# A hybrid decoder layer on one core: the opening's spread of c by transposes, and the recurrence gates as products over 64 rows, two halves of the channels at a time

## The chip, the core and the metric

The kernel runs on one core of a Trainium2 chip. Its time is the device time of one execution in microseconds. The engines are named as in the profile: PE (TensorE, matrix products; PEld are its weight loads), DVE (VectorE), ACT (ScalarE), POOL (GpSimd) and SP, which issues the DMA transfers. Times inside a profile are microseconds from the first instruction of the profiled execution.

## The reference, cut to what matters

One layer over x of 512 positions by 1024 channels, with a condition vector c of 1024. All data are float32.

```python
c_act = silu(c)
shift, scale, gate = split(c_act @ w_mod + b_mod, 3)
h = rmsnorm(x, norm_gain) * (1 + scale) + shift
q, k, v, z_attn, x_lru, z_lru = split(h @ w_in, 6)            # each 512 wide
attn = block_attention(rope(q), rope(k), v)                   # 8 heads of 64, causal
y_attn = rmsnorm(attn, attn_out_gain) * silu(z_attn)
xc = causal_depthwise_conv(x_lru, conv_w, conv_b)             # width 4
r = sigmoid(xc @ blockdiag(w_r) + b_r)                        # 8 blocks of 64 x 64
i = sigmoid(xc @ blockdiag(w_i) + b_i)
a = exp(-8 * r * softplus(-lam))
rec = scan(a, sqrt(1 - a * a) * i * xc)                       # h[t] = a[t] h[t-1] + u[t]
y_lru = rmsnorm(rec, lru_out_gain) * silu(z_lru)
out = rmsnorm(x + gate * (concat(y_attn, y_lru) @ w_out), final_gain)
```

## The kernel before

**Order.** Nothing is emitted where it is written. The function `op` records an operation with its engine, a cost, the buffers it reads and writes and a due time; `Plan.emit` (L97) then lays all operations out in one order per engine, with the costs as durations, taking at each engine the ready operation that is due first, and hands buffers out as they come free. The order on each engine is thus fixed when the program is built, and each engine's queue runs in that order. An operation with `alt` may go to either of two engines (PSUM copies to ACT or DVE). Constants such as `NWARM`, `SPACE`, `GATE0`, `DECAY0` shift due times. PSUM has 8 banks of 128 x 512; buffers marked "side" (scores, transposes, attention outputs, gate products) may hold at most 6 of them.

**Precision.** A product of two float32 matrices is done as three products of a high and a low part (`mm3`, L242 to L245): each operand is split by an ACT (or DVE) copy into the high part and a DVE subtraction into the low part (`split`, L247).

**Opening.** Eleven rows of 128 numbers (c and three columns of vectors) are loaded as `first`. ACT takes silu of the eight rows of c into `crow` (L320). PE turns `first` into columns (L325). For the modulation, silu(c) must stand in a row on all 128 partitions (`cb`): eight products of 8 contraction rows (L336), each with a column of the identity repeated 128 times, write it into two PSUM banks, which are copied out. `NWARM` products (L312) of a constant tile, whose result nobody reads, fill PE's queue until the first real work. Around them the queue holds four transposes (L416) of the first 128 channels of normalised x, one per 128 positions.

**First stage (L407 to L432).** For each of the 8 slices d of the channels: DVE multiplies the modulation weights by `cb` and sums along the row, which gives the two columns `g` (scale and shift; L384 for d = 0, L396 after); PE transposes x into a bank `xp` (L412); ACT makes `h = xp * scale + shift`, once as the high part (`h0h`, `h1h`, ...) and once whole, DVE the low part (`h0l`, ...); and PE does 21 products of 128 x 128 by 128 x 512 (L431) into seven banks `acc`. The weights `w0...` are split as above. Then 17 units follow (`UNITS`), each of 24 products for 128 further columns of the input projection (L693), `v` in one block of 96.

**Beside the units.** Attention runs in six blocks: scores (L570) as products over 32 rows, four of them on the four row strips of the array at a time, into four banks; softmax on DVE (L583) and ACT (L586, L597); transposes (L633) copied to `pt`; and the products with v (L616). The recurrence takes 4 chunks of 128 channels (two blocks of 64 each): `conv` (L487), then the two gates. Their weights `wg` are eight 128 x 128 matrices, one for each chunk and gate, each with two 64 x 64 blocks on its diagonal and zeros elsewhere. The gates are 3 products each (L500), so 24 in all, into a bank `gr` and a bank `gi` per chunk. ACT takes tanh of `gi` (L503); `gr` stays in its bank until `decay` (L509), which takes sigmoid of all four straight out of PSUM (L512) after one table load, and then the exponentials. `recur` does the scan.

**End.** The output projection (`po`), 16 groups of 12 products, is multiplied, added and normalised, and goes out.

Of the kernel before, what the change touches and what calls it, by code (L numbers as in the profile page):

```python
# [7 lines left out]
F32 = mybir.dt.float32  # L8
# [3 lines left out]
OP = mybir.AluOpType  # L12
# [9 lines left out]
NFIRST = 7  # L22
NWARM = 31
CUTS = (((0, 768), (768, 1024)), ((0, 512), (512, 1024)))
# [4 lines left out]
V_C = 72  # L29
NV = 80  # L30
UNITS = ["x3", "v0", "v1", "v2", "v3", "k2", "k3", "q2", "q3", "a0", "a1", "l0", "l1", "l2", "l3", "a2", "a3"]
SPACE = 14.0
BY_TANH = ("a0", "a1", "a2", "a3", "l0", "l1", "l2", "l3")
GATE0, GATE_STEP, DECAY0, REC0 = 32.0, 3.0, 44.0, 84.0

# [142 lines left out]
def tile_hymba_block(ctx: ExitStack, tc: tile.TileContext, x, ws0, wss, wgt, win0, wv, winr,  # L178
# [132 lines left out]
    for n in range(NWARM):  # L311
# [3 lines left out]

    epsc, ones, junk, crow = fix("epsc", [128, 1]), fix("ones", [128, 1]), fix("junk", [128, 1]), fix("crow", [ND, 128])
    op("V", 0.1, lambda: V.memset(epsc[:], EPS), [], [epsc], -20)
    op("V", 0.1, lambda: V.memset(ones[:], 1.0), [], [ones], 0)
    op("A", 0.1, lambda: A.activation(junk[:], epsc[:], AF.Silu), [epsc], [junk], -6, "silu")
    op("A", 0.1, lambda: A.activation(crow[:], first[0:ND, :], AF.Silu), [first, junk], [crow], -5, "silu")  # L320
    op("A", 0.1, lambda: A.activation(junk[:], epsc[:], AF.Sqrt), [epsc, crow], [junk], -4, "sqrt")


    ps, v0 = bank("v0"), fix("v0", [128, 3])
    op("PE", 0.2, lambda ps=ps: PE.transpose(ps[:, 0:11], first[:], ident[0:11, 0:11]), [first, ident], [ps], 1)  # L325
    op("V", 0.2, lambda ps=ps: (V.tensor_copy(v0[:, 0:2], ps[:, ND:ND + 2]), V.tensor_scalar(
        v0[:, 2:3], ps[:, ND + 2:ND + 3], 1.0, None, op0=OP.add)), [ps], [v0], 2)
    cb = t4("cb")
    for half in range(2):
        ps = bank("cp")  # L330
        s = slice(half * 512, (half + 1) * 512)

        def spread(ps=ps, half=half):
            for j in range(4):
                k = half * 4 + j
                PE.matmul(ps[:, j * 128:(j + 1) * 128], ident[0:ND, k:k + 1].to_broadcast([ND, 128]), crow[:], start=True, stop=True)  # L336
        op("PE", 0.8, spread, [crow, ident], [ps], 2)
        copy(512, lambda s=s: cb[:, s], lambda ps=ps: ps[:], [ps], [cb], 4.5 + 0.5 * half, True)
# [37 lines left out]
    def gain(d):  # L376

        sc, g = col("sc"), col("g")
        half = (sc, sch)
        for j in (1, 0):  # L380
            if d == 0:
                for n in range(2):
                    lo, up = CUTS[j][n]
                    op("V", dv(up - lo), lambda j=j, n=n, lo=lo, up=up: V.scalar_tensor_tensor(  # L384
                        ws[0][j][n][:], ws[0][j][n][:], 1.0, cb[:, lo:up], op0=OP.mult, op1=OP.mult,
                        accum_out=half[n][:, j:j + 1]), [ws[0][j][n], cb], [ws[0][j][n], half[n]], 8 - 2 * j + 0.7 * n)
                    if j and not n:
                        op("V", 0.1, lambda: V.tensor_add(sc[:, 1:2], sc[:, 1:2], v0[:, 2:3]), [sc, v0], [sc], 9.2)
                if j:
                    op("V", 0.2, lambda: V.tensor_scalar(g[:, 1:2], sch[:, 1:2], sc[:, 1:2], v0[:, 0:1],  # L390
                                                         op0=OP.add, op1=OP.mult), [sc, sch, v0], [g], 9.4)
                else:
                    op("V", 0.15, lambda: V.scalar_tensor_tensor(g[:, 0:1], sc[:, 0:1], v0[:, 1:2], sch[:, 0:1],
                                                                    op0=OP.add, op1=OP.add), [sc, sch, v0], [g], 9.5)
                continue
            op("V", dv(1024), lambda j=j: V.scalar_tensor_tensor(  # L396
                part(d, j), part(d, j), 1.0, cb[:], op0=OP.mult, op1=OP.mult, accum_out=sc[:, j:j + 1]),
               [ws[d][j], cb], [ws[d][j], sc])
        if d == 0:
            return g  # L400
        op("V", 0.2, lambda: V.tensor_scalar(
            g[:, 1:2], sc[:, 1:2], vec[:, V_SCALE + d:V_SCALE + d + 1], vec[:, V_GAIN + d:V_GAIN + d + 1],
            op0=OP.add, op1=OP.mult), [sc, vec], [g])
        op("V", 0.1, lambda: V.tensor_add(g[:, 0:1], sc[:, 0:1], vec[:, V_SHIFT + d:V_SHIFT + d + 1]), [sc, vec], [g])
        return g
# [81 lines left out]
    def conv(ps, ch, due, gate_due):  # L487
        xl, xc = t2("xl"), t2("xc")
        copy(512, lambda: xl[:], lambda: ps[:], [ps], [xl], due, True)
        w = lambda k: vec[:, V_CW + 4 * ch + k:V_CW + 4 * ch + k + 1]  # L490
        op("A", ac(512, 2), lambda: A.activation(xc[:], xl[:], AF.Identity, bias=vec[:, V_CB + ch:V_CB + ch + 1],
                                                 scale=w(3)), [xl, vec], [xc])
        for k in (2, 1, 0):
            s = 3 - k
            op("V", dv(512, 1), lambda k=k, s=s: V.scalar_tensor_tensor(  # L495
                xc[:, s:], xl[:, :S - s], w(k), xc[:, s:], op0=OP.mult, op1=OP.add), [xl, xc, vec], [xc])
        hi, lo = split(xc, t2, f"xc{ch}", 512)
        pr, pi, i = bank("gr", "side"), bank("gi", "side"), t2("gi")
        for ps2, n in ((pi, 2 * ch + 1), (pr, 2 * ch)):
            op("PE", 3 * pe(512), lambda n=n, ps2=ps2: mm3(  # L500
                ps2[:], wgs["h"][:, n], wgs["l"][:, n], hi[:], lo[:], True, True),
               [wgs["h"], wgs["l"], hi, lo], [ps2], gate_due + (0 if n % 2 else 2))
        op("A", acp(512, 1), lambda: A.activation(i[:], pi[:], AF.Tanh, bias=halves[:, ch:ch + 1], scale=0.5), [pi, halves], [i],  # L503
           gate_due + 2, "exp")
        op("V", dv(512), lambda: V.scalar_tensor_tensor(i[:], i[:], 1.0, xc[:], op0=OP.add, op1=OP.mult), [i, xc], [i],
           gate_due + 8)
        REC[ch] = (pr, i)

    def decay(chs, due):  # L509

        rs, prs = [t2("gr") for _ in chs], [REC[ch][0] for ch in chs]
        op("A", len(chs) * acp(512, 1), lambda: [A.activation(  # L512
            r[:], ps[:], AF.Sigmoid, bias=vec[:, V_BR + ch:V_BR + ch + 1]) for r, ps, ch in zip(rs, prs, chs)],
           [vec, *prs], rs, due, "sigmoid")
        for n, (r, ch) in enumerate(zip(rs, chs)):
# [180 lines left out]

    wgr = t4("wg", F32, (128, 8, 128))
    load(wgr, wg, T_REST + 2)
    wgs["h"], wgs["l"] = split(wgr, like(wgr), "wg", 1024)

# [22 lines left out]
    for u, name in enumerate(UNITS):  # L723
# [7 lines left out]
        elif kind == "x":  # L731
            conv(ps, idx, t1 + 1, T_REST + GATE0 + GATE_STEP * idx)
            decay(range(4), T_REST + DECAY0)
            for n in range(4):
# [180 lines left out]
```

## Time and profile before

| | |
|---|---|
| median of 3 runs | 238.06 us (237.94 to 239.41) |
| the profiled execution | 238.57 us, span 236.5 us |
| PE | 229.0 us busy (97%), 1236 products |
| DVE | 203.8 us busy (86%) |
| ACT | 139.3 us busy (59%) |
| POOL | 9.5 us busy (4%) |
| DMA | 38.54 MB, 163 GB/s over the span |

The span runs from the first to the last instruction; the device time is 2.07 us longer. A line of the timeline gives the start, the time that its instructions take together, the engine, the line of the kernel, the operation, and what it writes and reads; "x8" means eight instructions of that kind in a row. In the chain of waits each piece of time is given once, to the instruction that the end of the program waited for, so that its durations add up.

### The profile page before, as it was taken

To read this page: it belongs to the slowest core of one execution; us is meant where nothing else is said; L and a number is where in the kernel's file an instruction comes from. 1 tells how busy PE (TensorE), PEld (TensorE's weight loads), DVE (VectorE), ACT (ScalarE), POOL (GpSimd) and SP (SyncE) were. 2 spreads that over 40 slices of the span, in tenths; PEclk is the share of its full clock that TensorE was granted. 3 is DMA by queue.
4 is the path that set the end of the run, shared out by engine and by line. 5 is a ranking of instruction groups with operands and counts; after the bars stand their busy time and mean duration, and the time that the engine had idled before them with its cause. 6 is when DMAs were issued, how large, how long until landed. Compare 5 with 4: busy or idle time off the path is not lost.

```text
span 236.5 us, 3435 instructions
## 1 busy us (share of the span) xinstructions
PE 229.0 (97%) x1236; PEld 181.2 (77%) x1236; DVE 203.8 (86%) x396; ACT 139.3 (59%) x263; POOL 9.5 (4%) x32
## 2 busy tenths in 40 slices
PE   7999999999999999999999999999999999999990
PEld 5457888888888788786788887878887788888890
DVE  1679998895999899899999999989998999956583
ACT  7859464652659587799992347766374711303363
POOL 1010000057000000000000000000000000000000
PEclk9999999999999999999999999999999999999997
DMA  6999999822045223755122354474521000000044
GB/s 232 378 418 417 416 418 423 327 91 89 11 169 177 89 89 103 256 191 167 61 118 89 92 190 180 166 256 190 177 89 65 26 0 3 0 0 0 0 180 177
DMA packets 11782, 38.54 MB, mean 163 GB/s; under 512 B 1515, under 2 KB 1782, under 8 KB 11638
## 3 DMA queue, kind: packets, MB, share of 16 engines
q1 hardware_dynamic: 11600, 38.06, 43.5%
q10 hardware_dynamic: 166, 0.27, 0.3%
q8 instruction: 10, 0.16, 0.3%
q14 instruction: 6, 0.05, 0.1%
HBM read 36.22 MB, written 2.10 MB: 162 GB/s over the span
## 4 chain that ended last, share of the span: by engine, by line
PE 96%; ACT 1%; DVE 1%; issue 0%
PE acc L431 17%; PE pj L243 14%; PE pj L245 13%; PE pj L244 13%; PE po L243 6%; PE po L245 6%; PE po L244 6%; PE spare L312 4%; PE av L616 4%; PE sc L570 4%; PE tp L633 4%; PE cp L336 2%; PE xp L412 1%; PE ss L758 1%; PE gi L243 0%; PE gi L245 0%
## 5 line engine op out<-in xcount | busy, mean ns | idle before, releaser
L586 ACT ACTIVATE z<-z,mn 128x128 f32<-128x128 f32 (+3 forms) x32 | 17.7, 554 | 7.9 <-DVE mn L583 7.2
L396 DVE SCALAR_TENSOR_TENSOR ws<-ws,cb 128x1024 f32<-128x1024 f32 x14 | 16.9, 1219 | 0.4 <-DMA ws<-in_wss_dram 0.4
L583 DVE CUSTOM_DVE_ANT_0 z<-sc,cst 128x128 f32<-128x128 f32 (+3 forms) x32 | 14.2, 487 | 1.6 <-PE sc L570 1.6
L233 ACT COPY pt<-tp 128x128 f32<-128x128 f32 (+3 forms) x26 | 8.5, 391 | 6.2 <-PE tp L633 6.2
L312 PE MATMUL spare<-warm 128*128 128x512 bf16 x31 | 10.2, 486 | 1.5 <-DVE warm L310 1.5
L796 DVE SCALAR_TENSOR_TENSOR xr<-po,rba,xr 128x512 f32<-128x512 f32 (+2 forms) x9 | 6.2, 692 | 6.2 <-PE po L245 6.0
L807 ACT ACTIVATE o<-xr 128x512 f32<-128x512 f32 x7 | 4.4, 635 | 12.0 <-DVE xr L796 12.0
L633 PE MATMUL tp<-ident,z 128*128 128x128 f32 x80 | 10.5, 272 | 0.0
L633 PEld LDWEIGHTS tp<-ident,z 128*128 128x128 f32 x80 | 9.4, 140 | 1.4
L778 DVE TENSOR_TENSOR wo<-wo,grow 128x1024 f32<-128x1024 f32 x8 | 9.8, 1219 | 0.0
L541 DVE SCALAR_TENSOR_TENSOR wgt<-wgt,cb 128x1024 f32<-128x1024 f32 x8 | 9.7, 1218 | 0.0
L495 DVE SCALAR_TENSOR_TENSOR xc<-xl,vec,xc 128x511 f32<-128x511 f32 (+2 forms) x12 | 9.0, 747 | 0.2
L616 PE MATMUL av<-pt,v 128*64 128x512 f32 (+3 forms) x64 | 9.1, 436 | 0.0
L312 PEld LDWEIGHTS <-warm 128*128 128x128 bf16 x31 | 3.5, 118 | 6.1 <-issue 2.9
L616 PEld LDWEIGHTS av<-pt,v 128*64 128x64 f32 x64 | 4.3, 137 | 5.0 <-issue 4.1
L598 DVE TENSOR_SCALAR z<-z,sum 128x384 f32<-128x384 f32 (+3 forms) x20 | 7.2, 387 | 0.4
L233 ACT CAST wo21h<-wo 128x1024 fp32r<-128x1024 f32 x1 | 1.1, 1054 | 9.7 <-DVE wo L778 9.7
L657 ACT ACTIVATE sz<-pj 128x512 f32<-128x512 f32 x8 | 4.8, 599 | 3.3 <-PE pj L245 2.8
L419 ACT ACTIVATE h<-xp,g 128x512 f32<-128x512 f32 x8 | 6.2, 771 | 0.0
L597 ACT ACTIVATE z<-z,sum 128x128 f32<-128x128 f32 (+3 forms) x12 | 6.2, 546 | 0.0
L796 DVE SCALAR_TENSOR_TENSOR xr<-po,rbl,xr 128x512 f32<-128x512 f32 x8 | 6.0, 747 | 0.2
L586 ACT ACTIVATION_READ_ACCUMULATOR z<-z,mn 128x1 f32 x32 | 6.0, 188 | 0.0
(1121 smaller groups left out, 753.5 us busy)
## 6 DMA issues: line engine op xcount, KB each, us to landing
wc<-in_winr_dram SPq DMA_DIRECT2D x13, 512.0 KB, 3.3
ws<-in_wss_dram SPq DMA_DIRECT2D x4, 1024.0 KB, 11.1
wgt<-in_wgt_dram SPq DMA_DIRECT2D x8, 512.0 KB, 3.3
wo<-in_wo_dram SPq DMA_DIRECT2D x8, 512.0 KB, 3.4
w<-in_win_dram SPq DMA_DIRECT2D x7, 448.0 KB, 8.8
ws<-in_wss_dram SPq DMA_DIRECT2D x6, 512.0 KB, 6.4
x<-in_x_dram SPq DMA_DIRECT2D x4, 512.0 KB, 5.4
wv<-in_wv_dram SPq DMA_DIRECT2D x4, 512.0 KB, 3.8
```

Source lines behind the costliest of these rows:

```text
L243: PE.matmul(ps, lh, rh, start=start, stop=False)
L244: PE.matmul(ps, lh, rl, start=False, stop=False)
L245: PE.matmul(ps, ll, rh, start=False, stop=stop)
L312: op("PE", 0.32 if n < 11 else 0.235, lambda: PE.matmul(spare[:], warm[:, 0:128], warm[:], start=True, stop=True), [warm], [spare], 5.3 + ...
L396: op("V", dv(1024), lambda j=j: V.scalar_tensor_tensor(part(d, j), part(d, j), 1.0, cb[:], op0=OP.mult, op1=OP.mult, accum_out=sc[:, j:j + ...
L431: PE.matmul(acc[j][:], w[:, k * 128:(k + 1) * 128], b[:], start=first, stop=last),
L583: op("V", dv(n) + 0.085, lambda s=s, z=z, mn=mn: V.tensor_tensor_reduce(out=z[:, :n], in0=ps[s][:, cut], in1=cst[:, 2048 - n:2048], op0=OP ...
L586: op("A", ac(n, 1, 1), lambda s=s, z=z, mn=mn, sm=sm: A.activation(z[:, :n], z[:, :n], AF.Exp, bias=mn[:, 0:1], scale=-1.0, accum_out=sm[: ...
L616: PE.matmul(pss[u][64 * s:64 * s + 64, k * 128:], vt[k][:, h * 64:h * 64 + 64], pts[2 * u + s][:, k, k * 128:], start=(k == 0), stop=(k == 3))
L633: PE.transpose(at(h)[:, k * 128:(k + 1) * 128], z[:, k * 128:(k + 1) * 128], ident[:])
L778: op("V", dv(1024), lambda w=w, s=s: V.tensor_mul(w[:], w[:], grow[:, None, s].to_broadcast([128, 2, 512])), [w, grow], [w], t0 - 7 + 2 * j)
L796: op("V", dv(w, 1), lambda t=t, ps=ps, c0=c0, c1=c1, br=br: V.scalar_tensor_tensor(res[t][:, c0:c1], ps[:, :c1 - c0], rb[br][:, t:t + 1], ...
```

## The change

It has two parts, and constants that move due times with them.

- **Opening.** silu(c) is taken in place in `first`. The transpose of all eleven rows into columns now also delivers silu(c), copied whole to `v0` (one DVE copy; one plus the scale column is made by a separate small operation). `cb` is made by eight transposes of 128 x 128, each of one column of `v0` repeated 128 times. `NWARM` goes from 31 to 24.
- **Gates.** `wg` shrinks to four 128 x 128 matrices: in chunk ch, rows 0 to 63 hold the two blocks of the first 64 channels side by side (r in columns 0 to 63, i in 64 to 127), rows 64 to 127 those of the other 64 channels in the opposite order. The products take 64 rows each: the two halves of a chunk go to two banks, three products each, alternating between the upper and the lower half of the array's rows. There are still 24 products. They are recorded two chunks at a time, as one operation that takes four banks. Out of each bank 64 partitions are i (tanh on ACT, written to the other half's partitions) and 64 are r, which are copied to SBUF (ACT or DVE). `decay` reads r from SBUF.
- `SPACE` 14 to 13, `DECAY0` 44 to 56.

```diff
-NWARM = 31
+NWARM = 24
...
-SPACE = 14.0
+SPACE = 13.0
...
-GATE0, GATE_STEP, DECAY0, REC0 = 32.0, 3.0, 44.0, 84.0
+GATE0, GATE_STEP, DECAY0, REC0 = 32.0, 3.0, 56.0, 84.0
...
-    epsc, ones, junk, crow = fix("epsc", [128, 1]), fix("ones", [128, 1]), fix("junk", [128, 1]), fix("crow", [ND, 128])
+    epsc, ones, junk = fix("epsc", [128, 1]), fix("ones", [128, 1]), fix("junk", [128, 1])
     op("V", 0.1, lambda: V.memset(epsc[:], EPS), [], [epsc], -20)
     op("V", 0.1, lambda: V.memset(ones[:], 1.0), [], [ones], 0)
     op("A", 0.1, lambda: A.activation(junk[:], epsc[:], AF.Silu), [epsc], [junk], -6, "silu")
-    op("A", 0.1, lambda: A.activation(crow[:], first[0:ND, :], AF.Silu), [first, junk], [crow], -5, "silu")
-    op("A", 0.1, lambda: A.activation(junk[:], epsc[:], AF.Sqrt), [epsc, crow], [junk], -4, "sqrt")
-
-
-    ps, v0 = bank("v0"), fix("v0", [128, 3])
-    op("PE", 0.2, lambda ps=ps: PE.transpose(ps[:, 0:11], first[:], ident[0:11, 0:11]), [first, ident], [ps], 1)
-    op("V", 0.2, lambda ps=ps: (V.tensor_copy(v0[:, 0:2], ps[:, ND:ND + 2]), V.tensor_scalar(
-        v0[:, 2:3], ps[:, ND + 2:ND + 3], 1.0, None, op0=OP.add)), [ps], [v0], 2)
+    op("A", 0.1, lambda: A.activation(first[0:ND, :], first[0:ND, :], AF.Silu), [first, junk], [first], -5, "silu")
+    op("A", 0.1, lambda: A.activation(junk[:], epsc[:], AF.Sqrt), [epsc, first], [junk], -4, "sqrt")
+
+
+    ps, v0 = bank("v0"), fix("v0", [128, ND + 3])
+    op("PE", 0.3, lambda ps=ps: PE.transpose(ps[:, 0:ND + 3], first[:], ident[0:ND + 3, 0:ND + 3]), [first, ident], [ps], 1)
+    op("V", 0.15, lambda ps=ps: V.tensor_copy(v0[:], ps[:, 0:ND + 3]), [ps], [v0], 2)
+    one = fix("one", [128, 1])
+    op("V", 0.1, lambda: V.tensor_scalar(one[:], v0[:, ND + 2:ND + 3], 1.0, None, op0=OP.add), [v0], [one], 3)
...
-                PE.matmul(ps[:, j * 128:(j + 1) * 128], ident[0:ND, k:k + 1].to_broadcast([ND, 128]), crow[:], start=True, stop=True)
-        op("PE", 0.8, spread, [crow, ident], [ps], 2)
+                PE.transpose(ps[:, j * 128:(j + 1) * 128], v0[:, k:k + 1].to_broadcast([128, 128]), ident[:])
+        op("PE", 0.85, spread, [v0, ident], [ps], 2.5)
...
-        pr, pi, i = bank("gr", "side"), bank("gi", "side"), t2("gi")
-        for ps2, n in ((pi, 2 * ch + 1), (pr, 2 * ch)):
-            op("PE", 3 * pe(512), lambda n=n, ps2=ps2: mm3(
-                ps2[:], wgs["h"][:, n], wgs["l"][:, n], hi[:], lo[:], True, True),
-               [wgs["h"], wgs["l"], hi, lo], [ps2], gate_due + (0 if n % 2 else 2))
-        op("A", acp(512, 1), lambda: A.activation(i[:], pi[:], AF.Tanh, bias=halves[:, ch:ch + 1], scale=0.5), [pi, halves], [i],
-           gate_due + 2, "exp")
-        op("V", dv(512), lambda: V.scalar_tensor_tensor(i[:], i[:], 1.0, xc[:], op0=OP.add, op1=OP.mult), [i, xc], [i],
-           gate_due + 8)
-        REC[ch] = (pr, i)
+        REC[ch] = (xc, hi, lo, gate_due)
+
+    def gates(chs):
+
+        pss = {ch: [bank("g", "side") for _ in range(2)] for ch in chs}
+
+        def prods():
+            for ch in chs:
+                xc, hi, lo, _ = at[ch]
+                for c, (w_, x_) in enumerate((("h", hi), ("h", lo), ("l", hi))):
+                    for s in range(2):
+                        r = slice(64 * s, 64 * s + 64)
+                        PE.matmul(pss[ch][s][:], wgs[w_][r, 128 * ch:128 * ch + 128], x_[r, :], start=c == 0, stop=c == 2)
+        at = {ch: REC[ch] for ch in chs}
+        due = max(at[ch][3] for ch in chs)
+        op("PE", len(chs) * 3 * pe(512) + 0.3, prods, [wgs["h"], wgs["l"]] + [b for ch in chs for b in at[ch][1:3]],
+           [b for ch in chs for b in pss[ch]], due)
+        for n, ch in enumerate(chs):
+            xc, r, i = at[ch][0], t2("gr"), t2("gi")
+            own, other = [slice(0, 64), slice(64, 128)], [slice(64, 128), slice(0, 64)]
+            op("A", 2 * acp(512, 1), lambda ch=ch, i=i: [A.activation(
+                i[own[s]], pss[ch][s][other[s]], AF.Tanh, bias=halves[other[s], ch:ch + 1], scale=0.5) for s in range(2)],
+               [*pss[ch], halves], [i], due + 2 + n, "exp")
+            op("A", 2 * acp(512), lambda ch=ch, r=r: [A.copy(r[own[s]], pss[ch][s][own[s]]) for s in range(2)], pss[ch], [r],
+               due + 2 + n, alt=("V", 2 * dv(512), lambda ch=ch, r=r: [V.tensor_copy(r[own[s]], pss[ch][s][own[s]]) for s in range(2)]))
+            op("V", dv(512), lambda xc=xc, i=i: V.scalar_tensor_tensor(i[:], i[:], 1.0, xc[:], op0=OP.add, op1=OP.mult), [i, xc], [i],
+               due + 8 + n)
+            REC[ch] = (r, i)
 
     def decay(chs, due):
 
-        rs, prs = [t2("gr") for _ in chs], [REC[ch][0] for ch in chs]
-        op("A", len(chs) * acp(512, 1), lambda: [A.activation(
-            r[:], ps[:], AF.Sigmoid, bias=vec[:, V_BR + ch:V_BR + ch + 1]) for r, ps, ch in zip(rs, prs, chs)],
-           [vec, *prs], rs, due, "sigmoid")
+        rs = [REC[ch][0] for ch in chs]
+        op("A", len(chs) * ac(512, 1), lambda: [A.activation(
+            r[:], r[:], AF.Sigmoid, bias=vec[:, V_BR + ch:V_BR + ch + 1]) for r, ch in zip(rs, chs)], [vec, *rs], rs, due, "sigmoid")
...
-    wgr = t4("wg", F32, (128, 8, 128))
-    load(wgr, wg, T_REST + 2)
-    wgs["h"], wgs["l"] = split(wgr, like(wgr), "wg", 1024)
+    wgr = t2("wg")
+    load(wgr, wg, T_REST + 2, kb=256)
+    for n, t in zip("hl", split(wgr, t2, "wg", 512)):
+        wgs[n] = t
...
+            for chs in ((0, 1), (2, 3)):
+                gates(chs)
...
-    wg = np.zeros((128, 8, 128), f)
+    wg = np.zeros((128, 4, 128), f)
     for ch in range(4):
         for j, name in enumerate(("w_rgate", "w_igate")):
             for s in range(2):
                 b = slice(64 * s, 64 * s + 64)
-                wg[b, 2 * ch + j, b] = w[name][0, 2 * ch + s]
+                wg[b, ch, 64 * (j ^ s):64 * (j ^ s) + 64] = w[name][0, 2 * ch + s]
```

## Rows read from the trace of the kernel before

**Rows 1.** The profile's page: busy time of each engine, its share of the span, instructions.

```profile
PE 229.0 (97%) x1236; PEld 181.2 (77%) x1236; DVE 203.8 (86%) x396; ACT 139.3 (59%) x263; POOL 9.5 (4%) x32
```

**Rows 2.** The profile's page: the chain that ended last, by engine.

```profile
PE 96%; ACT 1%; DVE 1%; issue 0%
```

**Rows 3.** The chain of waits in order of time, from the start to the second channel slice: start, time, what.

```profile
1.54 1.89 PE spare L312 x4
3.42 0.21 PE v L325
3.63 3.61 PE cp L336 x16
7.24 3.52 PE spare L312 x8
10.77 0.21 PE xp L416
10.98 1.73 PE spare L312 x7
...
12.82 1.94 PE spare L312 x9
...
14.87 0.65 PE spare L312 x3
...
15.66 0.79 ACT h0h L419
...
16.49 6.96 PE acc L431 x28
...
23.89 4.82 PE acc L431 x21
```

**Rows 4.** The timeline of DVE, 13 to 20 us: start, time, instruction; in brackets the idle time before it and what ended it.

```profile
13.19 0.22 DVE L393 SCALAR_TENSOR_TENSOR g<-sc,v,sch 128x1 f32<-128x1 f32 x1
...
14.52 1.23 DVE L396 SCALAR_TENSOR_TENSOR ws<-ws,cb 128x1024 f32<-128x1024 f32 x1 [0.44 <-DMA ws<-in_wss_dram]
...
16.87 0.56 DVE L251 TENSOR_TENSOR w00384l<-w,w00384h 128x384 fp32r<-128x384 f32 x1 [1.12 <-ACT w00384h L233]
17.35 1.22 DVE L396 SCALAR_TENSOR_TENSOR ws<-ws,cb 128x1024 f32<-128x1024 f32 x1
...
18.49 0.69 DVE L421 TENSOR_TENSOR h0l<-h,h0h 128x512 fp32r<-128x512 f32 x1
...
19.50 0.15 DVE L404 TENSOR_TENSOR g<-sc,vec 128x1 f32<-128x1 f32 x1
```

**Rows 5.** The timeline of ACT, 11 to 21 us.

```profile
11.03 1.08 ACT L357 ACTIVATE xs<-x,ss 128x256 f32<-128x256 f32 x2
...
15.66 0.78 ACT L419 ACTIVATE h0h<-xp,g 128x512 fp32r<-128x512 f32 x1 [2.31 <-PE xp L416]
16.34 0.50 ACT L233 CAST w00384h<-w 128x384 fp32r<-128x384 f32 x1
...
20.74 0.77 ACT L419 ACTIVATE h1h<-xp,g 128x512 fp32r<-128x512 f32 x1
```

**Rows 6.** The timeline of PE, 19 to 22 us.

```profile
19.83 1.07 PE L431 MATMUL acc<-h0l,w00512h 128*128 128x512 f32 x4
...
21.56 0.73 PE L431 MATMUL acc<-h1h,w01h 128*128 128x512 f32 x2
```

**Rows 7.** The timeline of PE, 86 to 104 us: the first and the last of the 24 gate products.

```profile
87.10 0.48 PE L243 MATMUL gi<-xc0h,wgh 128*128 128x512 f32 x1
...
102.45 0.39 PE L245 MATMUL gr<-xc3h,wgl 128*128 128x512 f32 x1
```

**Rows 8.** The chain of waits at the attention scores of 512 columns: 24 products over 32 rows, of which 21 have a record, and the two full products behind them.

```profile
94.20 1.60 PE sc L570 x21
95.80 0.44 PE pj L243
96.24 0.23 PE pj L244
```

**Rows 9.** Groups of instructions by line, shapes kept apart: busy time in us, mean ns of one, idle time before them and what ended it. They are the tanh of the gates out of PSUM, and copies of a whole bank by ACT and by DVE.

```profile
L503 ACT ACTIVATE gi<-gi,halves 128x512 f32<-128x512 f32 x4 | 2.8, 690 | 1.3 <-PE gi L245 1.1
L233 ACT COPY xl<-acc 128x512 f32<-128x512 f32 x3 | 1.6, 597 | 6.1 <-PE acc L431 6.1
L234 DVE COPY at<-av 128x512 f32<-128x512 f32 x2 | 1.4, 690 | 0.0
```

**Rows 10.** The instructions on the gate weights, by line: duration in ns (smallest, median, largest), first and last start, shape.

```profile
L233 ACT CAST wgh<-wg x1: 1047/1047/1047, 66.2 to 66.2; 128x1024 fp32r<-128x1024 f32 x1
L251 DVE TENSOR_TENSOR wgl<-wg,wgh x1: 1221/1221/1221, 71.7 to 71.7; 128x1024 fp32r<-128x1024 f32 x1
```

**Rows 11.** Busy time by stretch: length, then busy time (instructions) of PE, PEld, DVE, ACT, POOL, granted PE clock, DMA share, GB/s.

```profile
66.00:98.00 32.00, 32.00 (x228) 25.69 (x227) 29.69 (x74) 24.27 (x59) 0.00 (x0) 1.00 0.40 136
98.00:122.00 24.00, 24.00 (x127) 18.25 (x126) 23.16 (x42) 23.20 (x36) 0.00 (x0) 1.00 0.44 154
122.00:210.00 88.00, 88.00 (x502) 70.77 (x502) 83.65 (x146) 42.33 (x88) 0.00 (x0) 1.00 0.30 102
```

**Rows 12.** The timelines of DVE and of PE where the first attention group ends: the last copies into pt and the first product that reads them.

```profile
107.14 1.28 DVE L234 COPY pt<-tp 128x512 f32<-128x512 f32 x2
...
109.32 1.08 PE L616 MATMUL av<-pt,v 128*64 128x512 f32 x4
```

More of the change, by code (lines that the diff above doesn't have):

```diff
@@ L387, in gain @@
                     if j and not n:
-                        op("V", 0.1, lambda: V.tensor_add(sc[:, 1:2], sc[:, 1:2], v0[:, 2:3]), [sc, v0], [sc], 9.2)
+                        op("V", 0.1, lambda: V.tensor_add(sc[:, 1:2], sc[:, 1:2], one[:]), [sc, one], [sc], 9.2)
                 if j:
-                    op("V", 0.2, lambda: V.tensor_scalar(g[:, 1:2], sch[:, 1:2], sc[:, 1:2], v0[:, 0:1],
+                    op("V", 0.2, lambda: V.tensor_scalar(g[:, 1:2], sch[:, 1:2], sc[:, 1:2], v0[:, ND:ND + 1],
                                                          op0=OP.add, op1=OP.mult), [sc, sch, v0], [g], 9.4)
                 else:
-                    op("V", 0.15, lambda: V.scalar_tensor_tensor(g[:, 0:1], sc[:, 0:1], v0[:, 1:2], sch[:, 0:1],
+                    op("V", 0.15, lambda: V.scalar_tensor_tensor(g[:, 0:1], sc[:, 0:1], v0[:, ND + 1:ND + 2], sch[:, 0:1],
                                                                     op0=OP.add, op1=OP.add), [sc, sch, v0], [g], 9.5)
@@ L880 @@
                 b = slice(64 * s, 64 * s + 64)
-                wg[b, 2 * ch + j, b] = w[name][0, 2 * ch + s]
+                wg[b, ch, 64 * (j ^ s):64 * (j ^ s) + 64] = w[name][0, 2 * ch + s]
     rows = [w["norm_gain"].reshape(8, 128), w["b_mod"].reshape(24, 128)[:16], w["b_mod"].reshape(24, 128)[16:].reshape(128, 8).T,
             w["conv_w"][0].reshape(4, 4, 128).transpose(1, 0, 2).reshape(16, 128),
-            w["conv_b"].reshape(4, 128), w["b_rgate"].reshape(4, 128), w["b_igate"].reshape(4, 128),
+            w["conv_b"].reshape(4, 128), w["b_rgate"].reshape(4, 128), w["b_igate"].reshape(4, 2, 64)[:, ::-1].reshape(4, 128),
             w["lru_lambda"].reshape(4, 128), w["attn_out_gain"].reshape(4, 128),
@@ L902 @@
         win0=c_(w_in[:, first].reshape(8, 128, 128 * NFIRST)), wv=wv, winr=c_(winr),
-        wo=c_(w["w_out"][0].reshape(2, 2, 2, 128, 2, 512).transpose(0, 4, 1, 3, 2, 5).reshape(8, 128, 2, 512)), wg=wg, vecs=vecs, top=c_(vecs.T[[*range(V_C, V_C + 8), V_GAIN, V_SHIFT, V_SCALE]]),
+        wo=c_(w["w_out"][0].reshape(2, 2, 2, 128, 2, 512).transpose(0, 4, 1, 3, 2, 5).reshape(8, 128, 2, 512)), wg=wg.reshape(128, 512), vecs=vecs, top=c_(vecs.T[[*range(V_C, V_C + 8), V_GAIN, V_SHIFT, V_SCALE]]),
         fgain=c_(w["final_gain"].reshape(1, 1024)), consts=tab)
```

## The prediction

> **What bounds the kernel now.** The page comes first: PE is busy for 97% of the span, DVE for 86% [rows 1], and the chain that ended last lies on PE for 96% [rows 2]. Busy is not the same as useful, so I read that chain in order of time [rows 3]. It has two parts. From 1.54 to 15.64 us PE runs the opening's queue, most of it products that nobody reads. From 16.49 us on it runs real products without a gap, and whatever leaves that stream shortens the run, as long as no operand comes late.
>
> In the opening, ACT waits 2.31 us for the last transpose of normalised x before it can make `h0h` [rows 5]. That transpose's input was ready at 11.03 + 1.08 = 12.11 [rows 5], and the columns `g`, the other input of `h0h`, at 13.19 + 0.22 = 13.41 [rows 4]. So the real work could have begun 15.66 - 13.41 = 2.2 us earlier; PE's queue held it. The chain also shows the clock: eight idle products from 7.24 take 3.52 us, 0.44 each, and nine from 12.82 take 1.94, 0.216 each [rows 3]. That is the 1.2 and the 2.4 GHz level; the rise falls in the group from 10.98, about 4.1 us after the spread ended. (The granted clock column shows 1.00 throughout, so the pitch is the better witness here.)
>
> **The change, part by part.**
>
> *Opening.* The spread was 3.61 us [rows 3]. Now it is eight transposes; one at the low level took 0.21 [rows 3], so 8 x 0.21 = 1.7, and 1.9 us leave the queue. In exchange there is a wait: the columns must exist first, so silu, the transpose of `first`, a copy by DVE and the spread follow each other. Behind that wait on PE stand only idle products and the x transposes; by the due times I place two idle products before the spread, which then ends near 6.5 instead of 7.24. DVE's next need of `cb` is the modulation weights, which come by load after 10 us, so the longer path costs nothing. The new copy and add on DVE lie in its early idle time.
>
> Seven idle products go: 7 x 0.216 = 1.5 us. After 6.5 us some 17 are left. If the clock rises 4.1 us after the spread, as before, at 10.6, about nine run at 0.43 and eight at 0.216; with the x transposes between them the queue ends near 12.7. If it rises 2.5 us later, near 14.0. Either way the binding input becomes `g` or the queue's end, and `h0h` starts at 13.5 to 14.0, the first real product 0.83 later, at 14.3 to 14.8.
>
> What is late next is DVE. Its first weights of slice 1 still come by load at 14.52 [rows 4], and end at 15.75. Then `w00384l` (0.48 to the next start), the second half of the weights (1.14) and `h0l` (0.69) [rows 4] end at 18.06; the 1.12 us for which DVE waited there [rows 4] is gone, since `w00384h` follows `h0h` on ACT. PE wants `h0l` 19.83 - 16.49 = 3.34 us after its first product [rows 3, 6], at 17.7 to 18.1: a wait of up to 0.4. Slice 1 then begins at 19.8 instead of 21.56 [rows 6]. Its `h1h` ended at 21.51 [rows 5], with no room; in the new order `g` for it is there at about 18.5 and ACT can end it by 19.3, or 20.2 if a scaling of x comes before it. I take **1.6 us** of gain. Ends: 2.2 (`h0h` at once, nothing late), and 0.7 if the second weights land only when they were used, at 17.35 [rows 4]; no gain at all if `h1h` stays where it was.
>
> *Gates.* Before, 24 full products: one slice of 21 takes 4.82 us [rows 3], 0.2295 each, so 5.51, between 87.10 and 102.45 [rows 7]. After, the same number over 64 rows, in pairs on the two halves of the array, each pair into two banks. No row shows products over 64 rows. The nearest does the like with four strips of 32 rows: 24 products of 512 columns, six rounds of four, take 1.60, and the next full product 0.44 in place of 0.23 [rows 8]. That is 1.60 + 0.21 = 1.81 for six rounds, of which 6 x 0.2295 = 1.38 is streaming and 0.43 the change to strips and back. Two chunks are also six rounds, so 2 x 1.81 = 3.62, and the gain is 5.51 - 3.62 = **1.9 us**. Ends: with nothing for the change of strips 2.75, a gain of 2.8; with no overlap at all 5.51 + 0.86, a loss of 0.9. I take the value of rows 8, since they show the same type, the same columns and the same alternation.
>
> *Evacuation.* Half of the partitions is no cheaper per instruction if time goes by columns, as I assume: eight tanh of 0.69 instead of four, and eight copies of 0.60 on ACT or 0.69 on DVE [rows 9]; 2.8 + 4.8 = 7.6 us more. The weights' split is halved, about 0.5 on ACT and 0.6 on DVE less [rows 10]. ACT is idle for 7.7 of the 32 us from 66 to 98, but for only 0.8 of the 24 after that, where DVE has 0.8 too [rows 11]. The later `DECAY0` moves a table load, the sigmoids and the exponentials out of the second stretch. PE has projection products to run meanwhile. I cost it at nothing, with that cover; without it, up to 7.6.
>
> *The rest.* Gate banks come free after the copy instead of after the sigmoid, which helps the scores, which need four. `SPACE` moves score blocks by 1 to 2 us among products that need nothing from them. The smaller load of `wg` is hidden. The end after the last product is unchanged. All these: 0.
>
> **Sum.** 1.6 + 1.9 = 3.5 us. The profiled execution took 238.57, so 235.1 on its scale; it lies 0.5 above the median, so **234.6** against 238.06. A difference of 1%, 2.4 us, is about what can be told from no change.
>
> **Rivals.**
>
> *The clock falls in the pause.* With fewer idle products PE may have little to do from 12.7 to 14.3, and much of that is transposes. Before, a pause of 16.49 - 15.64 = 0.85 did no harm [rows 3]; this one is about twice that. If the first real products run at the low level for the 4.1 us that the first rise took, they do 9 or 10 products that take 2.2 us at the high level: 1.9 lost, 236.5. Against it: the pause follows several microseconds at full pitch. Chance 0.10. The Trainium skill, "TensorE: Matmul & The Clock Gate", Part 4: PE-mode transpose, says that a transpose does not count as PE activity for the clock, and puts one at about 275 ns in a kernel. By that rule this rival gains weight, and the spread would come to an estimated 2.2 us; the trace has the transposes 0.21 apart even at the low level, and whether they hold the clock no row shows.
>
> *The halves don't overlap.* Then 238.06 - 1.6 + 0.9 = 237.3. Rows 8 speak against it. Chance 0.06.
>
> *The opening gives nothing*, because `h1h` or the loads hold slice 1 where it was: 238.06 - 1.9 = 236.2. For it: no room before `h1h`. Against it: DVE's 1.12 us of waiting before it. Chance 0.09.
>
> *ScalarE becomes the bound around the gates (slower).* A pair of chunks holds four of the six side banks until 4 tanh and 4 copies are done, 4 x 0.69 + 4 x 0.60 = 5.2 us on one engine. Scores and transposes queue for banks, `pt` is copied late, and PE stands at the attention product, behind which its whole queue waits. That product has little room now: the last copies end at 107.14 + 1.28 = 108.42, it starts at 109.32 [rows 12]. If all 7.6 us came through: 234.6 + 7.6 = 242.2. It ends above the time before when more than 3.5 of the 7.6 reach PE. For it: ACT's 23.20 of 24 us [rows 11]. Against it: the gates fall where ACT has idle time, copies may go to DVE, and decay moves behind. Chance 0.09 for slower by over 1%; another 0.06 that 1 to 3 us come through, 236 to 237.6.
>
> **Chances and range.** Forecast 0.60. Faster by over 1% (below 235.7) is the forecast, with a little of the others: 0.62. Within 1%: the clock, the missing overlap, the missing opening, the partial stall: 0.29. Slower: 0.09. Best ends 2.2 + 2.8 give 233.1; the range reaches from 233.3 up to 237.4, which takes in all cases but the slow one and the outermost ends.
>
> **What would show it.** Opening: `cp` near 1.7 us, ACT's wait for the x transposes under 1 us, `h0h` at 13.5 to 14.0, slice 1 at 19.8; half pitch after the first real product would be the clock rival. Gates: two blocks of 12 products with starts in pairs, each 1.6 us, the next product 0.44. Evacuation: no new idle time of PE before scores, transposes and attention products. I would be wrong if PE's stream had gaps after 20 us that add up to over 1 us.

## The result, and the profile after

The changed kernel takes 236.14 us (median of 4 runs, 235.12 to 236.30) against 238.20. The quotient of the two medians is 0.991; the ratio on record is 0.9886, with a 95% interval of 0.9857 to 0.9915, and the ratios given below are of that second kind. The kernel is faster, by 2.1 us by the medians and 2.7 by the ratio, where 3.5 were forecast; that is 0.9% or 1.1%, so it isn't settled whether the 1% of the forecast was reached. The time lies inside the range. It is 0.4 below the first rival's 236.5 (the clock) and next to the third's 236.2 (the opening gives nothing), so the time alone doesn't tell what happened. The profiled execution took 236.30 us, with a span of 234.2.

The page of the changed kernel, busy times and the chain by engine (before: [rows 1], [rows 2]):

```profile
PE 224.5 (96%) x1221; PEld 178.2 (76%) x1221; DVE 203.7 (87%) x396; ACT 150.0 (64%) x277; POOL 9.6 (4%) x32
PE 91%; DMA 3%; DVE 2%; ACT 1%; SPq 1%; issue 0%; ACTq 0%
```

PE's busy time fell by 4.5 us and ACT's rose by 10.7. The chain no longer starts in PE's queue: it now goes back through DVE to the load of the first modulation weights, so the idle products have left the path. The chain of waits through the opening (before: [rows 3]):

```profile
2.65 7.41 DMA ws<-in_ws_dram
...
13.16 0.23 DVE g L394
...
13.48 0.79 ACT h0h L420
...
14.31 8.16 PE acc L432 x28
...
22.91 4.80 PE acc L432 x21
```

`h0h` starts right behind `g`, 2.18 us earlier than before, as forecast. But the first 28 products take 8.16 us where they took 6.96 [rows 3]. The timeline of PE shows slice 1 at 20.72 instead of 21.56 [rows 6]:

```profile
9.70 1.24 PE L312 MATMUL spare<-warm 128*128 128x512 bf16 x5
11.42 0.33 PE L417 MATMUL xp<-ident,xs 128*128 128x128 f32 x1 [0.47 <-ACT xs L358]
12.14 0.33 PE L417 MATMUL xp<-ident,xs 128*128 128x128 f32 x1 [0.39 <-ACT xs L358]
12.30 0.60 PE L413 MATMUL xp<-ident,xs 128*128 128x128 f32 x4
14.31 2.08 PE L432 MATMUL acc<-h0h,w00512h 128*128 128x512 f32 x4 [1.41 <-ACT h0h L420]
...
20.72 0.84 PE L432 MATMUL acc<-h1h,w01h 128*128 128x512 f32 x3
```

The last five idle products start from 9.70 on, 0.216 us apart, so they are over at about 10.8. In the 3.5 us from there to the first real product PE does six transposes and otherwise waits. Four products then take 2.08 us. Busy time by stretch tells why (columns as in [rows 11]; the figure before the last two is the granted clock):

```profile
8.00:14.00 6.00, 4.03 (x21) 2.00 (x19) 4.34 (x15) 4.83 (x10) 0.00 (x0) 1.00 1.05 395
14.00:17.40 3.40, 3.09 (x7) 2.48 (x8) 2.93 (x7) 3.31 (x6) 1.09 (x1) 0.51 1.01 407
```

From 14.0 to 17.4 us the granted clock is 0.51, the 1.2 GHz level, and only seven products start there. This is the rival "the clock falls in the pause".

The gates, in the chain of waits (before: [rows 7]; the rows they were costed by: [rows 8]), and the first attention products behind them:

```profile
89.01 1.59 PE g L511 x11
90.60 0.43 PE pj L243
91.02 0.23 PE pj L244
...
97.42 1.59 PE g L511 x12
99.01 0.43 PE pj L243
...
105.78 4.71 PE av L634 x27
```

Each pair of chunks takes 1.59 us (twelve products, one of which has no record in the first) and the next product 0.43 in place of 0.23: the 1.81 of the forecast to 0.02. The attention block now takes 4.71 us. Before, in the chain of waits, it took 4.46:

```profile
109.39 4.46 PE av L616 x32
```

From 20 to 226 us PE has no idle time in this trace (206.00 of 206.00 us busy), so the gaps that would have shown the forecast wrong aren't there.

### The profile page after: what moved, and what is told of

Same layout as the page of the kernel before. It is cut to its first block, busy times and chain, and to the rows that moved or that the text cites. A ratio compares the mean times of both kernels' runs of the same rounds, so it can differ in the third digit from the quotient of the medians.

```text
span 234.2 us, 3421 instructions
## 1 busy us (share of the span) xinstructions
PE 224.5 (96%) x1221; PEld 178.2 (76%) x1221; DVE 203.7 (87%) x396; ACT 150.0 (64%) x277; POOL 9.6 (4%) x32
## 4 chain that ended last, share of the span: by engine, by line
PE 91%; DMA 3%; DVE 2%; ACT 1%; SPq 1%; issue 0%; ACTq 0%
PE acc L432 17%; PE pj L243 14%; PE pj L245 13%; PE pj L244 13%; PE po L243 6%; PE po L245 6%; PE po L244 6%; PE av L634 4%; PE sc L588 4%; PE tp L651 4%; DMA ws<-in_ws_dram 3%; PE g L511 1%; PE xp L413 1%; DVE ws L385 1%; PE ss L779 1%; SPq L240 1%
## 5 line engine op out<-in xcount | busy, mean ns | idle before, releaser
L601 DVE CUSTOM_DVE_ANT_0 z<-sc,cst 128x128 f32<-128x128 f32 (+3 forms) x32 | 14.3, 486 | 0.9 <-PE pj L244 0.5
L233 ACT COPY pt<-tp 128x128 f32<-128x128 f32 (+3 forms) x28 | 9.7, 405 | 5.5 <-PE tp L651 5.4
L634 PE MATMUL av<-pt,v 128*64 128x256 f32 (+3 forms) x64 | 9.3, 436 | 0.0
L312 PE MATMUL spare<-warm 128*128 128x512 bf16 x24 | 7.8, 468 | 1.5 <-DVE ones L318 1.5
L634 PEld LDWEIGHTS av<-pt,v 128*64 128x64 f32 x64 | 5.4, 137 | 4.1 <-issue 2.2
L496 DVE SCALAR_TENSOR_TENSOR xc<-xl,vec,xc 128x511 f32<-128x511 f32 (+2 forms) x12 | 8.4, 745 | 0.1
L616 DVE TENSOR_SCALAR z<-z,sum 128x128 f32<-128x128 f32 (+3 forms) x20 | 7.2, 383 | 0.4
L312 PEld LDWEIGHTS <-warm 128*128 128x128 bf16 x24 | 2.5, 113 | 4.2 <-DVE ones L318 1.5
L523 DVE COPY gr<-g 64x512 f32<-64x512 f32 x6 | 4.1, 688 | 1.7 <-ACT gi L519 1.6
```

The lines of the kernel that those rows point to most:

```text
L312: op("PE", 0.32 if n < 11 else 0.235, lambda: PE.matmul(spare[:], warm[:, 0:128], warm[:], start=True, stop=True), [warm], [spare], 5.3 + ...
L601: op("V", dv(n) + 0.085, lambda s=s, z=z, mn=mn: V.tensor_tensor_reduce(out=z[:, :n], in0=ps[s][:, cut], in1=cst[:, 2048 - n:2048], op0=OP ...
L634: PE.matmul(pss[u][64 * s:64 * s + 64, k * 128:], vt[k][:, h * 64:h * 64 + 64], pts[2 * u + s][:, k, k * 128:], start=(k == 0), stop=(k == 3))
```

## Experiments: the opening

Clock figures below are the mean granted clock of one execution. A stretch of 3.4 us at half the clock, as from 14.0 to 17.4 above, takes about 1.7 / 234 = 0.007 off that mean. Where no fall is counted below, the mean is 0.991 or more; with one it is 0.984 to 0.989. The fall itself is seen in the four traces of executions that have it; in the others it is read off the mean.

**The opening alone**, on the gates, `SPACE` and `DECAY0` of before.

> The opening of the changed kernel (spread by transposes, 24 idle products) on the gates, SPACE and DECAY0 of the kernel before. Theory A, the clock falls in the pause: the first real product starts near 14.3 us instead of 16.5, at half pitch in most executions; slice 1 of the first stage begins near 20.7 instead of 21.56, and the time is 0.8 to 1.0 us below the kernel before, about 237.3. Executions in which the clock doesn't fall are some 1.1 us faster and show a mean clock of about 0.99 or more in place of 0.985. Rival B, the first stage is held by operands (DVE, loads) and the clock is only a witness: slice 1 begins near 20.7 in every execution and the executions don't fall into two groups.

Measured: 236.59 us (6 runs), ratio 0.9908 (0.9890 to 0.9927). One execution of six shows the fall, 0.987 and 237.40 us; the other five, 0.992 to 0.994, have a median of 236.56. The one execution with the fall is thus 0.8 us slower than the rest, as theory A says, but the fall was rarer than expected ("most executions"), and the opening alone gave 2.3 us instead of 0.8 to 1.0, for that reason as far as the record shows.

**The gates alone**, on the opening of before.

> The gates over 64 rows, with SPACE 13 and DECAY0 56, on the opening of the kernel before (31 idle products, the spread by eight products). If the two parts add up: the opening as before, first real product near 16.5 us at full pitch, two blocks of gate products of 1.6 us, and 1.8 us below the kernel before, about 236.4. If the gates' evacuation cost something that the shorter opening hid: less than 1.3 us below.

Measured: 237.59 us (9 runs), ratio 0.9949 (0.9929 to 0.9970): 1.2 us, with an interval of 0.7 to 1.7. The time meets the second expectation (less than 1.3 us), and the interval leaves out the 1.8 of the first. In its trace the stretch from slice 1 to the last product is 1.5 us shorter than before, between the two, and the attention block again takes about a quarter of a microsecond more than before, which the last section of experiments takes up.

**Six idle products in the pause.**

```diff
+    for n in range(6):
+        op("PE", 0.235, lambda: PE.matmul(spare[:], warm[:, 0:128], warm[:], start=True, stop=True),
+           [warm], [spare], 13.0 + 0.1 * n, lat=0.0, after=12.3)
```

> The changed kernel with six more idle products, placed in the pause between the transposes of slice 1 and the first real product; nothing else moves. Theory A, the clock falls because PE is nearly idle there: it now holds, the first real product starts near 14.3 us at full pitch (0.23 us), slice 1 begins near 19.8, and the time is some 0.9 us below the changed kernel, about 235.2, in all executions. Rival B (operands hold slice 1 near 20.7): no change, 236.1. If the idle products delay the first real one: slower by up to 0.3 us.

Measured: 234.98 us (5 runs), ratio 0.9843 (0.9821 to 0.9865), and no execution below 0.994. The stretch of the clock, and PE's timeline:

```profile
14.00:17.40 3.40, 3.33 (x14) 2.43 (x14) 3.19 (x6) 3.22 (x5) 1.05 (x1) 1.00 1.02 406
```

```profile
12.30 1.46 PE L315 MATMUL spare<-warm 128*128 128x512 bf16 x6
13.88 1.19 PE L435 MATMUL acc<-h0h,w00512h 128*128 128x512 f32 x4
...
19.44 0.84 PE L435 MATMUL acc<-h1h,w01h 128*128 128x512 f32 x3
```

Fourteen products start where seven did, and slice 1 begins 5.56 us after the first real product instead of 6.41. (The first real product itself came 0.43 us earlier in this execution than in the changed kernel's; that part isn't the clock's.) Work that nobody reads, put where nothing waits for it, makes this stretch shorter: the pause and not the operands had taken the time. For the whole time this one comparison isn't enough, since the two intervals overlap; the counts further down settle it.

**Twelve transposes in the pause** instead of six products.

> As the run with six more idle products in the pause, but the pause is filled by twelve transposes of 128 x 128 of the identity, 0.11 us each, about the same stretch of PE time. If transposes keep the clock up as products do: first real product at full pitch and about 235.2. If a transpose doesn't count for the clock: half pitch after 14.3 us as in the changed kernel, and about 236.1.

Measured: 235.13 us (5 runs), ratio 0.9839 (0.9817 to 0.9861), no execution below 0.993. Transposes do as well as products. But the opening alone had shown the fall once in six on that chip, so this did not yet tell the two theories apart.

**The changed kernel again, a longer pause, and a longer pause filled with transposes.** `NWARM` 24 to 16 for the second; for the third also:

```diff
+    for n in range(28):
+        op("PE", 0.1175, lambda: PE.transpose(spare[:, 0:128], ident[:], ident[:]),
+           [ident], [spare], 9.78 + 0.14 * n if n < 16 else 13.0 + 0.05 * n, lat=0.0, after=0.0 if n < 16 else 12.3)
```

> The changed kernel once more, on the chip of the next two runs. Theory: its executions fall into two groups, about 235.1 (mean clock 0.993 or more, no fall of the clock after the first rise) and about 236.2 (0.989 or less, a fall near 14 us), in shares that no trace lets me foresee.

> The changed kernel with 16 idle products instead of 24: PE has only six of the x transposes between about 9 and 14.3 us. Theory A (the clock falls because PE is nearly idle): it falls before the first real product in every execution, mean clock 0.989 or less, 236.2 or more. If the length of the pause doesn't matter: as the changed kernel, in two groups.

> The kernel with 16 idle products, and 28 transposes of the identity (0.11 us each) where the eight products were and in the pause. From about 9 to 14 us PE does transposes alone. If transposes hold the clock as products do: no fall, about 235. If a transpose doesn't count for the clock: as the kernel with 16 idle products and no transposes, 236.2 or more, with a fall in every execution.

Measured, the changed kernel: 235.44 us (5 runs), ratio 0.9862 (0.9835 to 0.9889). Two executions with the fall, 236.53 and 235.94 at 0.988 and 0.984; three without, 234.90 to 235.44 at 0.995 to 0.997. With the first four runs that is five of nine with the fall, median 236.28, and four without, median 235.08: **the fall costs 1.2 us**.

Longer pause: 237.02 us (6 runs), ratio 0.9921 (0.9892 to 0.9950). All six show the fall by their mean clock (0.976 to 0.989), as expected; two of the times, 235.49 and 236.19, lie below the 236.2 that was expected at least. Four are at 0.978 or less and above 236.8: as I read that mean, the clock was low there for about twice as long. The one trace of this kernel is of the execution with 236.19 us, and no trace of the other kind was kept. With transposes: 235.16 us (4 runs), ratio 0.9854 (0.9829 to 0.9879), none below 0.993. Its timeline and its clock:

```profile
8.73 0.60 PE L315 MATMUL spare<-ident 128*128 128x128 f32 x4
...
9.28 1.47 PE L315 MATMUL spare<-ident 128*128 128x128 f32 x12
...
12.64 1.47 PE L315 MATMUL spare<-ident 128*128 128x128 f32 x12
14.21 0.96 PE L435 MATMUL acc<-h0h,w00512h 128*128 128x512 f32 x3
```

```profile
14.00:17.40 3.40, 3.30 (x16) 2.55 (x14) 2.93 (x7) 3.28 (x6) 1.08 (x1) 1.00 1.03 411
```

From 8.73 us to the first real product PE did nothing but transposes, and the clock held. So transposes in the pause served as well as products.

Counted over all runs, those of the next section too: with the pause filled, by products or by transposes, no execution of 44 shows the fall; with the pause open it is 12 of 21 (5 of 9 of the changed kernel, 1 of 6 with the opening alone, 6 of 6 with the longer pause). One rival is left, that the fall depends on how early the clock had risen, which differs between executions. Two traces answer it. In that of the changed kernel's second set and in that of the run `halves_apart` of the next section the clock rose equally late, by the first idle products behind the spread:

```profile
6.53 1.75 PE L312 MATMUL spare<-warm 128*128 128x512 bf16 x6
```

```profile
6.53 1.76 PE L312 MATMUL spare<-warm 128*128 128x512 bf16 x6
```

With the pause open the clock then fell, with it filled it held:

```profile
14.00:17.40 3.40, 3.08 (x7) 2.48 (x8) 2.89 (x5) 3.23 (x6) 1.09 (x1) 0.51 1.03 410
```

```profile
14.00:17.40 3.40, 3.38 (x14) 2.47 (x14) 3.20 (x6) 3.26 (x5) 1.07 (x1) 1.00 1.02 410
```

## Experiments: the gates

All of these have the six idle products in the pause, so that the clock doesn't blur them; they stand against that run's ratio of 0.9843.

**The order of the six products of a chunk**: three of one half, then three of the other.

```diff
-                for c, (w_, x_) in enumerate((("h", hi), ("h", lo), ("l", hi))):
-                    for s in range(2):
+                for s in range(2):
+                    for c, (w_, x_) in enumerate((("h", hi), ("h", lo), ("l", hi))):
```

> The changed kernel with six idle products in the pause, and the gate products in another order: the three of one half of the rows first, then the three of the other, so that neighbours no longer alternate between the halves. Theory: the gain of the gates is the overlap of the two halves; without it each block takes 12 x 0.23 + 0.2 = 2.9 us instead of 1.6, and the time is some 2.2 us (two halves still meet once per chunk) to 2.6 us above the run with six more idle products. If the gain came from freed banks or from the shifted due times: no change.

Measured: 235.24 us (4 runs), ratio 0.9858 (0.9834 to 0.9882): no change, a miss. But the trace shows that the experiment didn't take the overlap away: the products still start in pairs 0.00 to 0.01 us apart and a block still takes 1.6 us. The half that stands later in the program runs beside the half that stands first. So it says nothing about the cause of the gain, and the next one was built to keep the halves apart.

**The halves as two operations**, with full products between them.

```diff
+        for s in range(2):
+            op("PE", len(chs) * 3 * pe(512) + 0.3, lambda s=s: prods(s), [...],
+               [pss[ch][s] for ch in chs], due + 4.0 * s)
```

(`[...]` stands for the inputs, which are the same. Tanh and the copies of r are due 5 us later in this run, and DVE's operation on the result of tanh 3 us later.)

> The changed kernel with six idle products in the pause, and the gate products of the upper and the lower halves of the rows as two operations, due 4 us apart, with full products between them, so that the two halves can't meet. Tanh and copies wait for both. Theory: the gain of the gates is that the halves overlap. Without it four blocks of six products take 4 x 1.81 = 7.2 us of PE instead of 3.6, and the time is 3.6 us above the run with six idle products, near 238.6, a little above the kernel before it. If the gain came from freed banks or shifted due times: no more than 1 us above.

Measured: 238.17 us (12 runs), ratio 0.9983 (0.9968 to 0.9998). The chain of waits:

```profile
87.73 1.59 PE g L513 x6
...
93.87 1.58 PE g L513 x6
...
97.04 1.58 PE g L513 x6
...
103.35 1.59 PE g L513 x6
104.93 4.46 PE av L637 x32
```

Four blocks instead of two, each as long as one with both halves: six products of one half take what twelve of both did. The loss is 1.4% of the time, 3.3 us, where 3.6 were expected. The first block stands next to the scores and the last next to the attention products, which need strips too, so each saves a change of strips, 0.2 us; and the attention block takes 4.46 us instead of 4.71. In the traces that leaves 3.0 us, and 2.9 are found from slice 1 to the last product (210.28 against 207.34). The gain of the gates is the overlap.

**One chunk at a time.**

```diff
-            for chs in ((0, 1), (2, 3)):
+            for chs in ((0,), (1,), (2,), (3,)):
```

> As the run with six idle products in the pause, but the gates one chunk at a time instead of two: four blocks of three rounds. Theory: each block pays 0.43 us for the change to half rows and back, so two more blocks cost 0.86 us of PE, 0.6 to 0.9 above the run with six idle products. If the change of strips were free: no difference; if freeing two banks earlier helped, up to 0.3 below.

Measured: 235.24 us (4 runs), ratio 0.9859 (0.9836 to 0.9883), 0.4 us more but within the intervals. In its trace the blocks take 0.89 each, four of them 3.56 instead of 3.18, and one of them stands next to the scores, as the chain of waits shows:

```profile
85.93 0.89 PE g L514 x6
...
89.08 0.89 PE g L514 x5
89.97 1.60 PE sc L591 x22
...
103.28 4.48 PE av L637 x32
```

The direction is the expected one, about half as large. Of the 0.86, 0.2 is saved where a block adjoins the scores and shares the change of strips with them, and 0.23 by the attention block, which took 4.48 us here instead of 4.71.

**Every copy of r twice.**

> As the run with six idle products in the pause, but every copy of r out of PSUM is done twice, 8 x 0.6 to 0.7 = 5 us more for ACT and DVE. Theory A (the evacuation is covered by projection products, but for 0.25 us): less than 0.8 us above the run with six idle products. Rival B (ACT and DVE set the time around the gates): 2 to 5 us above, with new idle time of PE before transposes or attention products.

Measured: 236.55 us (6 runs), ratio 0.9915 (0.9893 to 0.9937): 1.7 us above, between the two. The timelines of PE and of DVE around the second score block show where:

```profile
92.70 1.61 PE L592 MATMUL sc<-k0h,q0h 32*128 32x512 f32 x8
93.92 0.85 PE L592 MATMUL sc<-k0l,q0h 32*128 32x512 f32 x8
```

```profile
90.34 2.85 DVE L527 COPY gr<-g 64x512 f32<-64x512 f32 x4 [0.43 <-ACT gi L522]
```

The scores need four banks; DVE's doubled copies out of the gate banks end at 93.19, and the block, begun at 92.70, takes 2.47 us instead of 1.60. That is half of the 1.7. The rest comes long after the gates, in places such as this score block, which takes 1.60 in the run with six idle products:

```profile
163.12 1.89 PE sc L592 x17
```

The order of the operations differs there too, so the experiment doesn't show how much of the rest the copies cost as such. About a third of the 5 us came through in all: the cover that I named for the evacuation is real, and it isn't complete.

**The copies into `pt` ahead of the gates' evacuation** (tanh due 4 us later, copies of r 6 us).

> As the run with six idle products in the pause, but tanh and the copies of r are due 4 and 6 us later, so that the copies into pt for the first attention group don't stand behind them on ACT. Theory: the first attention products start in pairs again (0.01 us apart instead of 0.26) and their block takes 4.46 us instead of 4.71; the time is 0 to 0.3 us below the run with six idle products. If the pairing has another cause: the block stays at 4.7.

In the changed kernel the timeline of ACT before the first attention block shows what stands ahead of those copies:

```profile
102.70 1.39 ACT L519 ACTIVATE gi<-g,halves 64x512 f32<-64x512 f32 x2
104.12 1.19 ACT L522 COPY gr<-g 64x512 f32<-64x512 f32 x2
105.33 1.07 ACT L233 COPY pt<-tp 128x512 f32<-128x512 f32 x2
```

The block's second operand, the first of the two copies in the last line, is thus written until 105.9; its products start 0.26 us apart instead of in pairs 0.01 apart, and stay out of step for the whole block. Measured with the new due times: 234.66 us (4 runs), ratio 0.9839 (0.9813 to 0.9865), and in the chain of waits

```profile
107.23 4.46 PE av L637 x32
```

The pairs are back, and with them the 0.25 us of the block. The whole time can't be told from the run without this edit. Still, this version, the one with idle products alone and the one with transposes in their place have ratios of 0.9839 to 0.9843, against 0.9886 and 0.9862 of the two sets of the changed kernel: 0.5 to 1.1 us less.

## Why the prediction was right, and where it was off

**What bounds the kernel: right.** PE's stream set the time, the opening's queue had held it, and `g` became the binding input: `h0h` at 13.48 and the first real product at 14.31, for 13.5 and 14.3 at the early end. DVE ended `h0l` at 18.02, for 18.06.

**Opening, 1.6 us: right only while the clock holds.** The step that failed is the length of PE's queue. I let the clock rise 4.1 us after the spread, as before, and had the queue end at 12.7 or later. It rose within a microsecond of the spread's end, at about 7.3 us in this trace, and in the other traces with transposes too; the remaining idle products ran at 0.216 and were over at 10.8. So the pause was not 1.6 us but 3.5, with six transposes in it, and the rival to which I gave 0.10 came in five of nine executions. The pause before, which I set beside it as 0.85 us, held four transposes, and PE's idle time in it was 0.43. The rival's price, 1.9, was too high: 1.2 measured. With the clock held PE waits 0.4 for `h0l`, and the fall covers that wait; the traces show 0.85 of the 1.2 before slice 1 (6.41 against 5.56 us), and where the rest lies isn't shown. In the profiled execution the opening gave 21.56 - 20.72 = 0.84. In the eight traces with the pause filled, slice 1 began between 19.17 and 19.99, 5.5 to 5.6 us after a first real product between 13.62 and 14.49; so the opening gave 1.6 to 2.4, median 2.05, a little more than the forecast's 1.6.

**Gates, 1.9 us: right in the mechanism, 0.4 too large.** The products themselves came out as costed from rows 8. From the first projection product to the last product of all, PE takes 172.7 us before and with the opening alone, and 171.2 with the gates alone and in the changed kernel: 1.5 less. (From slice 1 on the changed kernel is 1.8 shorter, but 0.2 of that lies in the first stage, ahead of the gates.) Of the 0.4 that is missing, 0.25 is the attention block; where the rest lies isn't shown.

**Evacuation, nothing: nearly.** A quarter of a microsecond came through, at the very product that the slow rival named (little room before the attention products), and the doubled copies, some 5 us more, cost 1.7. Half of the partitions was no cheaper, as assumed: a tanh took 684 ns, for 690 [rows 9]. The rise of 10.7 us on ACT isn't the tanh and the copies of r alone. Six of the eight copies of r went to DVE, as its line on the page shows,

```profile
L523 DVE COPY gr<-g 64x512 f32<-64x512 f32 x6 | 4.1, 688 | 1.7 <-ACT gi L519 1.6
```

and other operations moved from DVE to ACT, among them two copies into `pt` (four of this size on ACT now, two before). So the slow rival was a matter of degree, and it came by a copy that had changed its engine.

**Sum.** When the clock holds, the change gives about the 3.5 us: 3.7 with the pause filled by six products (1.57% of 238.2), and 3.1 and 3.5 in the changed kernel's executions without the fall (one of the first set, three of the second, each against the median before of its set). That the sum comes so near is in part luck, since the opening gave 0.4 more than costed and the gates 0.4 less. The 1.2 us of the fall, in the executions that have it, make up most of the rest.

The Trainium skill, "TensorE: Matmul & The Clock Gate", Part 4: PE-mode transpose, says that the full clock doesn't engage for transposes, which don't count as busy time of PE in the same way. The run with transposes alone from 8.73 us to the first real product kept the clock at 1.00, where six of six executions without them lost it. The measurement decides: here transposes held the clock as products did.

## What to carry to other kernels

Idle work at the start of a kernel has two ends: too much of it delays the first real product, too little leaves a pause in which the clock may fall; put it behind the last early work, up to the moment when the first real operand lands, rather than only ahead. When a product uses half of the contraction rows, pair it with one on the other half, two banks each, and gather such pairs into few blocks; then look at who empties the banks, since that is where the next wait appears. And when executions of one kernel differ by half a per cent, set the granted clock of each beside its time before anything else is made of a median.

## What the hardware showed that I had not expected

- The eight products over 8 contraction rows before, 3.61 us of a busy PE [rows 3], were followed by some 4 us at the low level, in both kept traces that have them; eight transposes in their place by less than 1 us, in all twelve. No experiment tells which difference between the two spreads does it.
- Products on the two halves of the rows overlap (pairs 0.00 to 0.01 us apart) even when three on one half stand in the program before the first on the other.
- Two streams of products on column halves that start 0.26 us apart, as here where one operand was late, stay apart to the end of their block: 4.71 us instead of 4.46.
